# A hybrid SSD and pooling block: state products in plain fp32, silu in the convolution, inverse square roots as one GpSimd power

## The chip, the cores and the metric

The kernel runs on one core of one Trainium2 chip. The metric is the time on the device in microseconds (us), the median of three runs. The profile is of one further execution. Engines are named as in it: PE is TensorE (PEld its weight loads), DVE is VectorE, ACT is ScalarE, POOL is GpSimd, SP is SyncE, whose queue issues the loads.

## The reference

All arrays are fp32: 2048 latent tokens and 256 context tokens of 1024 channels. Cut to what matters here:

```python
x = layer_norm(x, emb_ln_g, emb_ln_b)
z, xbc, dt_raw, up = split_projection(modulate(x, sh1, sc1), in_proj)
xbc = silu(depthwise_conv_centred(xbc, conv_w, conv_b))     # x (1024), B (128), C (128)
# per direction, chunks of 128 tokens, 16 heads of 64:
y_diag = scores @ x                                         # inside a chunk
states = B^T (x * w_end);  h = h * chunk_decay + states     # from chunk to chunk
y_off  = (C h) * exp(a_cum)
y   = rms_norm((y_fwd + y_bwd + d_skip * x) * silu(z), ssd_norm_g)
mix = concat([y, pool_mixer(up)]) @ w_out
x   = layer_norm(ALPHA * x + g1 * mix, ln1_g, ln1_b)
ffn = (silu(h @ w_gate) * (h @ w_up)) @ w_down              # h = modulate(x, sh2, sc2)
x   = layer_norm(ALPHA * x + g2 * ffn, ln2_g, ln2_b)
```

The context goes through the same projection, convolution and scan first; its final states start the scans of the latent tokens.

## The kernel before

Nearly all products are made of three matmuls: each operand is split into a part rounded to fp32r and the rest, and `mm3` (L74) adds high times high, high times low and low times high. The split costs a cast on ACT and a subtraction on POOL or DVE for each operand. Plain fp32 products, one call of `mm` (L71) on unsplit operands, are used for the context's states and, in the scan, for chunks 0, 14 and 15 (`exact`, L1146).

The stages in order of time, with the rough stretch of the trace:

- 0 to 180 us: modulation rows, context, LayerNorms of the latent tokens (`ln_h`, L231) a step at a time between the blocks of a contraction. Each pair of token tiles needs one inverse square root (L247).
- 180 to 450 us: projection of B, C, dt and x. `x_block` (L805) makes a block of 128 channels for four groups of 512 tokens. `conv_main` (L594) copies the projection from PSUM (L601), `conv` (L368) makes the first tap on POOL (L373) and four more on DVE (L375), and on B, C and the context a silu on ACT (L377). The x blocks of the latent tokens go to `conv_tok` (L617) without silu, two blocks later, are transposed on PE and stored token-major in `xbc_d`. Beside the first two x blocks runs `dt_stage` (L766), which uses Exp on ACT.
- 450 to 840 us: u and its pooling, z, the decayed scores (`Scores`, L664).
- 840 to 1070 us, phase 2: from the last chunk to the first the pooled part of the output projection (48 matmuls of 512 columns a chunk, L1112) and the backward state. `prep` (L1065) loads x and B of the next chunk, applies silu (L1083, ACT), the end weights (L1084, POOL), and splits them (L1086 and L1087 on ACT, L1088 and L1089 on POOL). `add_state` (L385) makes two products a chunk.
- 1070 to 1510 us, phase 3: for every chunk `scan_y` (c+1), `scan_in` (c+2), `to_ffn` (c-1), `out_proj` (c). `scan_in` (L1142) loads C, x, the stored backward state, scores and z, applies silu to x (L1161), splits C, both states, B and the weighted x (L1152 to L1171, L1189 to L1192) and makes six products: two of `add_state`, and C times either state for each half of the channels (L1201, L1202). `scan_y` (L1210) adds the scores' product, gates, and splits y. `out_proj` (L1238) makes 48 matmuls, and needs two inverse square roots: of the mean square (L1251), without which its PSUM can't be emptied (L1252), and of the LayerNorm (L1258), without which the chunk can't go on to `to_ffn`.
- 1510 to 2500 us: gate and up projections as seven block products, prepared by ACT, POOL and DVE.
- 2500 us to the end: down projection; in its last sixteen slots of 33 matmuls each the second LayerNorm of a chunk (`finish`, L1576), with one inverse square root (L1583).

`rsqrt` (L82) is a guess from the exponent's bits and three Newton steps on tiles of one or two columns: eleven DVE instructions with one column (L88, L89, three times L94, twice L99, L102, L103), thirteen with two. There are 9 + 2 x 16 + 16 = 57 calls.

The tile framework orders each engine's instructions ahead of time from its own simulated timeline (`schedule_with_timeline_sim=True`, L1704), not as they are written. Engines work through their queues in that order. Buffers: in phase 3 three PSUM banks for `ps_mm`, two for transposes, three for `ps_ss`.

Of the kernel before, what the change touches and what calls it, by code (L numbers as in the profile page):

```python
# [21 lines left out]
H = 16  # L22
# [13 lines left out]
def hybrid_block_kernel(ctx: ExitStack, tc: tile.TileContext, a: dict, out: bass.AP, dbg=None):  # L36
# [45 lines left out]
    def rsqrt(v, n, tag):  # L82
        """[P, n] tile of v ** -0.5: a guess from the exponent bits and Newton's steps."""
        v_ = nc.vector
        i = small.tile([P, n], I32, tag=tag + "i", name=tag + "i")
        r = small.tile([P, n], F32, tag=tag + "r", name=tag + "r")
        t = small.tile([P, n], F32, tag=tag + "t", name=tag + "t")
        v_.tensor_scalar(out=i, in0=v.bitcast(I32), scalar1=1, scalar2=None, op0=ALU.logical_shift_right)  # L88
        v_.tensor_scalar(out=r.bitcast(I32), in0=i, scalar1=-1.0, scalar2=float(0x5F3759DF), op0=mult, op1=add)  # L89
        s = 1.0  # L90
        for step in range(3):
            # r is s times the guess, s a power of two
            if n == 1:
                v_.scalar_tensor_tensor(out=t, in0=r, scalar=v, in1=r, op0=mult, op1=mult)  # L94
            else:
                v_.tensor_tensor(out=t, in0=r, in1=r, op=mult)
                v_.tensor_tensor(out=t, in0=t, in1=v, op=mult)
            if step < 2:
                v_.scalar_tensor_tensor(out=r, in0=t, scalar=-3.0 * s * s, in1=r, op0=add, op1=mult)  # L99
                s = -2.0 * s ** 3  # L100
            else:
                v_.tensor_scalar(out=t, in0=t, scalar1=-0.5 / s ** 3, scalar2=1.5 / s, op0=mult, op1=add)  # L102
                v_.tensor_tensor(out=r, in0=r, in1=t, op=mult)  # L103
        return r
# [70 lines left out]
    class AdaRows:  # L175
        """Rows g * 2048 .. of the modulation as a chain of steps of kq blocks of the contraction."""
# [54 lines left out]
    def ln_h(src, t0, r, tp, parts, o, keep):  # L231
        """Two token tiles from row t0: columns o .. o+256 of the parts; a generator, a channel block at a time."""
# [84 lines left out]
    def atanh2(s, z, q):  # L317
        """s = 2 artanh(z), |z| <= 1/3, by its series; a generator, to be run a few instructions at a time."""
# [9 lines left out]
    def softplus(x, n, tp):  # L328
        """x [P, n, 32] <- softplus(x + dt_bias) = max(v, 0) + log1p(exp(-|v|)); a generator."""
# [38 lines left out]
    def conv(dst, raw, n, blk, act=True):  # L368
        """dst[:, j] = sum_d w[d] raw[:, j + d] + b for the 128 channels of block blk, then silu."""
# [6 lines left out]
        if act:  # L376
            nc.scalar.activation(out=dst, in_=dst, func=AF.Silu)  # L377
# [7 lines left out]
    def add_state(hn, hp, dec, xw, bt, low=None):  # L385
        """hn = hp * decay + B^T (x * w); both [P(n), 1024]; low: the operands' low parts."""
        if hp is not None:
            nc.vector.tensor_tensor(out=heads(hn), in0=heads(hp), in1=bch(dec), op=mult)
        for g in range(2):
            ps = ps_ss()  # L390
            s = slice(g * 512, (g + 1) * 512)
            if low is not None:
                mm3(ps, lambda k: bt, lambda k: low[1], lambda k: xw[:, s], lambda k: low[0][:, s], 1)
            else:
                mm(ps, bt, xw[:, s], True, True)
# [5 lines left out]
    # ==== phase 1: modulation, context, and the projections =====================================  # L401
# [58 lines left out]
    class Ahead:  # L460
        """The LayerNorms of the latent tokens, a step at a time, each one's loads and statistics during the one before."""
# [22 lines left out]
    def tick(n, m=0):  # L484
        """Every n blocks of a contraction, a step of the LayerNorms ahead."""
# [82 lines left out]
    def ctx_states():  # L568
        """The final states of the context's scans."""
# [24 lines left out]
    def conv_main(st, s, ps, blk):  # L594
# [14 lines left out]
        conv(cv[:, j0:j1], raw[:, j0:], j1 - j0, blk, blk >= 8)  # L609
# [54 lines left out]
    class Scores:  # L664
        """Both scans' decayed scores of the chunks, [j, (i block, h, i)], which depend on B, C and dt alone, and the skip.

        A product over 128 rows makes the exponents: running sums at i, what belongs to j, and the mask.
        Rows j >= 64 hold the block of their own i first.
        """
        def __init__(self, kp):  # L670
# [13 lines left out]
            # the skip's weight of each head where i is j, in the places of the scores  # L684
# [28 lines left out]
        def step(self):  # L713
            """Two groups of four heads."""
# [33 lines left out]
    def log(out_, x, tp):  # L748
        """out_ = ln x for x > 0: the exponent and 2 artanh((m - 1) / (m + 1)) of the mantissa m; a generator."""
# [16 lines left out]
    def dt_stage():  # L766
        with pool("dtp", "right") as dtp:
# [15 lines left out]
            for i in range(2):  # L783
                for d in range(2):
                    for half in range(2):
# [6 lines left out]
                        if i == 0:  # L792
                            # rows of the product, blocks of its columns, half of i
# [55 lines left out]
    def pool_block(u, w, ci):  # L849
# [20 lines left out]
        # rows  # L870
# [64 lines left out]
    def pooled_weights(w2s):  # L935
        """The pooling mixer's maps times the output projection's rows and the gate; a generator, in 16 blocks."""
# [89 lines left out]
    # modulation of the second sub-layer, folded with the first LayerNorm's affine part  # L1026
# [6 lines left out]
    # ==== phase 2: pooled part of the output projection; backward states =========================  # L1033
# [31 lines left out]
    def prep(c):  # L1065
# [9 lines left out]
        xh = xl = None  # L1075
        if c > 0:
            xl = b3.tile([P, D + P], F32R, tag=f"xt{c % 2}", name="xt")
            xt = f32(xl)
            if c >= NCH - 2:
                after(xl)  # L1080
# [627 lines left out]
```

## Time and profile before

| what | value |
|---|---|
| median of 3 runs | 2827.87 us (2825.07 to 2831.69) |
| profiled execution, its span from first to last instruction | 2824.6 us |
| PE busy | 2628.3 us, 93% of the span, 11886 matmuls |
| DVE busy | 1995.0 us, 71% |
| POOL busy | 1466.0 us, 52% |
| ACT busy | 979.3 us, 35% |
| DMA | 454.92 MB, mean 161 GB/s |

Of the profiled execution only the span is known, so its own time is taken as the span; the median of the runs lies 3.3 us above it. Busy shares are means over stages that differ. A matmul record's duration covers its way through the array, and records overlap, so what a matmul costs is read from the spacing of starts.

### The profile page before, as it was taken

The page shows a single profiled execution, that of the slowest core. Times are in us where ns is not written, and L with a number is a line of the kernel's source. Part 1 is how long each engine was busy: PE and PEld are TensorE (multiplying, and loading weights), DVE is VectorE, ACT ScalarE, POOL GpSimd, SP SyncE. Part 2 cuts the span into 40 slices and gives each one's busy share as a digit, 9 for nine tenths or more (in the row PEclk, how much of TensorE's full clock was granted, in tenths as well). Part 3 has the DMA queues.
Part 4 walks back from the last instruction along what each step waited for, and adds up shares of the span by engine and source line. Part 5 has one row for each costly group of instructions (what it writes and reads, how often), then busy time and mean ns, then how long its engine had stood idle before and what let it go on. Part 6 is the DMA issues. An engine that isn't in the chain of part 4 may idle for free.

```text
span 2824.6 us, 34660 instructions
## 1 busy us (share of the span) xinstructions
PE 2628.3 (93%) x11886; PEld 2091.9 (74%) x11886; DVE 1995.0 (71%) x2775; ACT 979.3 (35%) x1701; POOL 1466.0 (52%) x1177
## 2 busy tenths in 40 slices
PE   7989999999998898888898999998999998999996
PEld 3557788788876676666677888886888887888775
DVE  4767755856547886999988677678755555546787
ACT  2543221125533323444444322224333324333332
POOL 4554423424436786566644555555555553415366
PEclk9989999999999999999999999998999999999998
DMA  9722421137765666455565455545533327555643
GB/s 317 258 72 67 123 68 55 67 108 196 185 184 201 205 208 213 164 196 182 182 216 194 146 180 179 166 166 197 176 113 103 109 90 227 153 160 177 192 145 102
DMA packets 392456, 454.92 MB, mean 161 GB/s; under 512 B 31173, under 2 KB 287920, under 8 KB 388952
## 3 DMA queue, kind: packets, MB, share of 16 engines
q1 hardware_dynamic: 298016, 340.29, 38.7%
q10 hardware_dynamic: 93784, 112.30, 11.3%
q8 instruction: 94, 1.54, 0.2%
q14 instruction: 82, 0.67, 0.1%
q0 software_dynamic: 480, 0.11, 0.1%
HBM read 294.34 MB, written 158.28 MB: 160 GB/s over the span
## 4 chain that ended last, share of the span: by engine, by line
PE 29%; DVE 13%; issue 6%; POOL 4%; DMA 4%; ACT 2%; ACTq 0%; SPq 0%; POOLq 0%; DVEq 0%
PE b L72 28%; POOL x L1375 1%; DMA h<-hid_d 1%; PE mm L72 1%; DVE h L1415 1%; DVE h L1287 1%; DVE r2t L94 1%; DVE r1t L94 1%; POOL cs L1439 1%; DMA hid_d<-hs 1%; DVE xl L1192 1%; DVE sil L1235 1%; DVE ev L1388 1%; DMA wdr<-in_w_down 0%; DVE ryt L94 0%
## 5 line engine op out<-in xcount | busy, mean ns | idle before, releaser
L72 PE MATMUL b<-wd,h 128*128 128x512 f32 x1848 | 427.8, 394 | 16.5 <-ACT h L1414 7.6
L72 PEld LDWEIGHTS b<-wd,h 128*128 128x128 f32 x1848 | 351.1, 190 | 93.0 <-ACT h L1414 8.0
L72 PE MATMUL mm<-HT,wh 128*128 128x512 f32 x832 | 329.4, 398 | 3.8 <-ACT u L926 2.9
L72 PE MATMUL mm<-LT,wh 128*128 128x512 f32 x832 | 329.0, 395 | 0.0
L72 PE MATMUL mm<-HT,wl 128*128 128x512 f32 x832 | 327.7, 395 | 0.0
L1388 DVE TENSOR_TENSOR ev<-ev,b 128x512 f32<-128x512 f32 x301 | 200.8, 680 | 117.8 <-PE b L72 97.3
L1375 POOL TENSOR_TENSOR x<-cs,x 128x512 fp32r<-128x512 f32 x132 | 181.1, 1372 | 178.9 <-ACT x L1374 164.2
L1415 DVE TENSOR_TENSOR h<-h 128x768 fp32r<-128x768 f32 x112 | 134.9, 1214 | 125.5 <-ACT h L1414 121.0
L72 PEld LDWEIGHTS mm<-HT,wh 128*128 128x128 f32 x832 | 158.4, 190 | 38.2 <-ACT u L926 3.3
L72 PEld LDWEIGHTS mm<-LT,wh 128*128 128x128 f32 x832 | 158.1, 190 | 32.7 <-issue 0.7
L72 PEld LDWEIGHTS mm<-HT,wl 128*128 128x128 f32 x832 | 157.7, 189 | 32.8 <-issue 0.3
L1374 ACT CAST x<-cs 128x512 fp32r<-128x512 f32 x176 | 108.8, 621 | 184.0 <-PE b L72 67.5
L375 DVE SCALAR_TENSOR_TENSOR cv<-raw,vt,cv 128x512 f32<-128x512 f32 (+2 forms) x160 | 129.2, 819 | 59.7 <-POOL cv L373 56.8
L1375 POOL TENSOR_TENSOR x<-wraw,x 128x512 fp32r<-128x512 f32 x44 | 62.4, 1419 | 188.0 <-ACT x L1374 124.2
L1414 ACT CAST h<-h 128x768 fp32r<-128x768 f32 x112 | 87.0, 782 | 209.0 <-DMA h<-hid_d 186.8
L1374 ACT CAST x<-wraw 128x512 fp32r<-128x512 f32 x132 | 79.1, 620 | 187.5 <-PE b L72 98.8
L283 POOL TENSOR_TENSOR wl<-wraw,wh 128x1024 fp32r<-128x1024 f32 (+1 forms) x35 | 81.1, 2319 | 112.9 <-ACT wh L280 108.8
L72 PE MATMUL mm<-WyH,yh 128*128 128x512 f32 x256 | 109.2, 426 | 19.4 <-DVE bs L1252 16.7
L72 PE MATMUL b<-y0h,x 128*128 128x512 f32 x344 | 115.4, 397 | 5.5 <-ACT y0h L1334 5.5
L72 PE MATMUL b<-y1h,x 128*128 128x512 f32 x344 | 114.0, 393 | 3.6 <-ACT y1h L1334 3.6
L72 PE MATMUL b<-y4h,x 128*128 128x512 f32 x344 | 114.4, 394 | 0.0
L72 PE MATMUL b<-y3h,x 128*128 128x512 f32 x344 | 113.3, 390 | 0.0
(469 smaller groups left out, 6778.9 us busy)
## 6 DMA issues: line engine op xcount, KB each, us to landing
wraw<-in_w_gate SPq DMA_DIRECT2D x44, 512.0 KB
wraw<-in_w_up SPq DMA_DIRECT2D x44, 512.0 KB
hid_d<-ev ACTq DMA_DIRECT2D x88, 256.0 KB
h<-hid_d SPq DMA_DIRECT2D x56, 384.0 KB
tw_d<-wdr SPq DMA_DIRECT2D x77, 256.0 KB
wd<-tw_d SPq DMA_DIRECT2D x77, 256.0 KB
wada<-in_w_ada SPq DMA_DIRECT2D x72, 256.0 KB
wraw<-in_in_proj SPq DMA_DIRECT2D x35, 512.0 KB
```

What stands on the lines that cost most here:

```text
L72: nc.tensor.matmul(ps, lhsT=lhsT, rhs=rhs, start=start, stop=stop)
L94: v_.scalar_tensor_tensor(out=t, in0=r, scalar=v, in1=r, op0=mult, op1=mult)
L283: nc.gpsimd.tensor_tensor(out=wl[:, split:], in0=raw[:, split:], in1=f32(wh[:, split:]), op=sub)
L375: nc.vector.scalar_tensor_tensor(out=dst, in0=raw[:, d:d + n], scalar=w(d), in1=dst, op0=mult, op1=add)
L1192: nc.vector.tensor_tensor(out=xl, in0=xw, in1=f32(xh), op=sub)
L1235: nc.vector.tensor_reduce(out=sq, in_=y.rearrange("p k t -> p t k"), axis=mybir.AxisListType.X, op=add)
L1287: nc.vector.tensor_tensor(out=tt[i], in0=x, in1=y, op=sub)
L1374: nc.scalar.copy(h, src)
L1375: (nc.vector if i % 3 == 0 else nc.gpsimd).tensor_tensor(out=l, in0=src, in1=f32(h), op=sub)
L1388: nc.vector.tensor_tensor(out=o, in0=t, in1=ps, op=add)
L1414: nc.scalar.copy(th, f32(tl))
L1415: nc.vector.tensor_tensor(out=tl, in0=f32(tl), in1=f32(th), op=sub)
```

## The change

Three edits; comments and docstrings go too.

1. The state products of phases 2 and 3 take their operands unsplit, in plain fp32: `exact`, the splits and the low parts are gone. In `prep` the weighted x gets a buffer for even and one for odd chunks.
2. `conv` always ends in silu, so `xbc_d` holds silu of x, and the silus in `prep` and `scan_in` go.
3. `rsqrt` is one POOL instruction, a power with a constant tile of -0.5.

```diff
     def rsqrt(v, n, tag):
-        v_ = nc.vector
-        i = small.tile([P, n], I32, tag=tag + "i", name=tag + "i")
         r = small.tile([P, n], F32, tag=tag + "r", name=tag + "r")
...
+        nc.gpsimd.tensor_tensor(out=r, in0=v, in1=mhalf[:, 0:n], op=ALU.pow)
         return r
...
+    mhalf = cst.tile([P, 2], F32, name="mhalf")
+    nc.gpsimd.memset(mhalf, -0.5)
...
-        if act:
-            nc.scalar.activation(out=dst, in_=dst, func=AF.Silu)
+        nc.scalar.activation(out=dst, in_=dst, func=AF.Silu)
...
-            if low is not None:
-                mm3(ps, lambda k: bt, lambda k: low[1], lambda k: xw[:, s], lambda k: low[0][:, s], 1)
-            else:
-                mm(ps, bt, xw[:, s], True, True)
+            mm(ps, bt, xw[:, s], True, True)
...
-        conv(cv[:, j0:j1], raw[:, j0:], j1 - j0, blk, blk >= 8)
+        conv(cv[:, j0:j1], raw[:, j0:], j1 - j0, blk)
...
-            xs = b3.tile([P, D], F32, tag="xs", name="xs")
-            nc.scalar.activation(out=xs, in_=xt[:, 0:D], func=AF.Silu)
-            nc.gpsimd.tensor_tensor(out=heads(xs), in0=heads(xs), in1=bch(wend[:, c, H:2 * H]), op=mult)
-            xh = b3.tile([P, D + P], F32R, tag="xh", name="xh", bufs=1)
-            nc.scalar.copy(xh[:, 0:D], xs)
-            nc.scalar.copy(xh[:, D:D + P], xt[:, D:D + P])
-            nc.gpsimd.tensor_tensor(out=xl[:, 0:D], in0=xs, in1=f32(xh[:, 0:D]), op=sub)
-            nc.gpsimd.tensor_tensor(out=xl[:, D:D + P], in0=xt[:, D:D + P], in1=f32(xh[:, D:D + P]), op=sub)
+            xs = b3.tile([P, D], F32, tag=f"xs{c % 2}", name="xs")
+            nc.gpsimd.tensor_tensor(out=heads(xs), in0=heads(xt[:, 0:D]), in1=bch(wend[:, c, H:2 * H]), op=mult)
...
-        if not exact:
-            cth = se.tile([P, P], F32R, tag="cth", name="cth", bufs=2)
-            nc.scalar.copy(cth, ctk)
-            nc.gpsimd.tensor_tensor(out=ctl, in0=ctk, in1=f32(cth), op=sub)
-            hfh = so.tile([P, 2, 512], F32R, tag="y0h", name="hfh", bufs=2)
-            hfl = so.tile([P, 2, 512], F32R, tag="y0l", name="hfl", bufs=2)
-            h2 = hf.rearrange("p (g x) -> p g x", g=2)
-            nc.scalar.copy(hfh, h2)
-            nc.gpsimd.tensor_tensor(out=hfl, in0=h2, in1=f32(hfh), op=sub)
...
-        nc.scalar.activation(out=xt[:, 0:D], in_=xt[:, 0:D], func=AF.Silu)
...
-                xl = so.tile([P, 2, 512], F32R, tag="y0l", name="xl", bufs=2).rearrange("p g x -> p (g x)")
-                nc.scalar.copy(bh, xt[:, D:D + P])
-                nc.scalar.copy(xh, xw)
-                nc.vector.tensor_tensor(out=bl, in0=xt[:, D:D + P], in1=f32(bh), op=sub)
-                nc.vector.tensor_tensor(out=xl, in0=xw, in1=f32(xh), op=sub)
-                add_state(hn, hf, cdec[:, c, 0:H], xh, bh, (xl, bl))
+            add_state(hn, hf, cdec[:, c, 0:H], xw, xt[:, D:D + P])
...
-                mm3(pf, lambda k: cth, lambda k: ctl, lambda k: hfh[:, g], lambda k: hfl[:, g], 1)
-                mm3(pb, lambda k: cth, lambda k: ctl, lambda k: hbh[:, g], lambda k: hbl[:, g], 1)
+            mm(pf, ctk, hf[:, n], True, True)
+            mm(pb, ctk, hb[:, n], True, True)
```

## Rows read from the trace of the kernel before

**Rows 1.** Stretches: us, busy us (instructions) of PE, PEld, DVE, ACT, POOL, PEclk, DMA, GB/s
```profile
1186.00:1391.00 205.00, 171.72 (x925) 135.46 (x925) 197.38 (x319) 93.64 (x167) 130.49 (x79) 0.93 0.57 189
873.00:1046.00 173.00, 154.36 (x622) 122.25 (x621) 144.34 (x125) 51.66 (x77) 134.90 (x60) 0.94 0.61 208
250.00:450.00 200.00, 195.97 (x913) 157.08 (x912) 128.40 (x173) 49.21 (x100) 71.43 (x103) 1.00 0.32 89
620.00:830.00 210.00, 205.03 (x942) 168.79 (x941) 111.23 (x160) 104.19 (x214) 83.74 (x82) 0.99 0.67 186
```
**Rows 2.** Silus at the head of scan_in, ACT by time: start us, us
```profile
1186.62 1.05 ACT L1161 ACTIVATE xt<-xt 128x1024 f32<-128x1024 f32 x1
...
1391.12 1.07 ACT L1161 ACTIVATE xt<-xt 128x1024 f32<-128x1024 f32 x1
```
**Rows 3.** Waits of PE, 1186 to 1391 us: us in total, times, longest
```profile
PE mm L72 <- DVE bs L1252: 13.4, 6, 3.7
```
**Rows 4.** DVE groups, 1186 to 1391 us: busy us, mean ns, idle before
```profile
L1192 DVE TENSOR_TENSOR xl<-t,xh 128x1024 fp32r<-128x1024 f32 x8 | 18.1, 2260 | 0.0
L94 DVE SCALAR_TENSOR_TENSOR r1t<-r1r,ve 128x1 f32<-128x1 f32 x24 | 16.3, 677 | 0.7
...
L1191 DVE TENSOR_TENSOR bl<-xt,bh 128x128 fp32r<-128x128 f32 x8 | 5.5, 681 | 0.1
...
L88 DVE TENSOR_SCALAR ryi<-ssq 128x1 int32<-128x1 int32 x8 | 1.2, 148 | 0.1
```
**Rows 5.** A small DVE instruction beside a POOL one, by time: start us, us
```profile
1206.56 2.37 POOL L1171 TENSOR_TENSOR hbp<-hbp,hbh 128x1024 fp32r<-128x1024 f32 x1
1206.66 2.29 DVE L99 SCALAR_TENSOR_TENSOR ryr<-ryt,ryr 128x1 f32<-128x1 f32 x1
```
**Rows 6.** POOL groups, 1186 to 1391 us, then 873 to 1046 us
```profile
L1158 POOL TENSOR_TENSOR hfl<-hf,hfh 128x1024 fp32r<-128x1024 f32 x8 | 21.4, 2674 | 0.8 <-ACT hfh L1157 0.8
...
L1088 POOL TENSOR_TENSOR xt<-xs,xh 128x1024 fp32r<-128x1024 f32 x12 | 34.1, 2840 | 5.6 <-ACT xh L1086 5.6
```
**Rows 7.** PE by time: two plain fp32 products of the context's states (four records)
```profile
318.79 1.88 PE L72 MATMUL ss<-cxw,xtc 128*128 128x512 f32 x4
320.50 0.38 PE L624 MATMUL tr<-con,cv 128*128 128x128 f32 x2
```
**Rows 8.** PE by time: one split product (three records) and what follows it
```profile
1220.70 0.39 PE L72 MATMUL ss<-hfh,cth 128*128 128x512 f32 x1
...
1221.39 0.82 PE L1270 MATMUL tr<-con,bs 128*128 128x128 f32 x6
```
**Rows 9.** POOL, smallest arithmetic of two columns, whole span: busy us, mean ns
```profile
L252 POOL TENSOR_SCALAR stat<-nm 128x2 f32<-128x2 f32 x8 | 2.2, 281 | 5.3 <-DVE rst L96 2.7 <-DVE nm L249 2.5
```
**Rows 10.** PE by time, end of phase 3: waits in brackets
```profile
1486.27 1.97 PE L1270 MATMUL tr<-con,bs 128*128 128x128 f32 x8 [6.36 <-DVE ryr L89]
...
1512.72 1.41 PE L1270 MATMUL tr<-con,bs 128*128 128x128 f32 x8 [4.61 <-DVE bs L1259]
```
**Rows 11.** Waits of PE, 830 to 1070 us
```profile
PE ss L72 <- DVE hb L397: 8.5, 3, 3.4
PE ss L72 <- POOL xt L1088: 5.5, 4, 2.8
...
PE ss L72 <- ACT xh L1087: 2.7, 3, 1.1
```
**Rows 12.** The end of the kernel by time: last matmuls, then chunk 15's LayerNorm
```profile
2792.74 6.05 PE L72 MATMUL b<-wd,h 128*128 128x512 f32 x26
...
2809.50 0.68 DVE L1643 TENSOR_TENSOR acc<-acc,b 128x512 f32<-128x512 f32 x1
...
2816.31 0.21 DVE L1584 TENSOR_SCALAR nm<-mv,r2r 128x1 f32<-128x1 f32 x1
```
**Rows 13.** POOL in the last slots by time
```profile
2803.56 2.48 POOL L1588 TENSOR_TENSOR acc<-acc,ln_g_t 128x512 f32<-128x512 f32 x2 [2.02 <-ACT acc L1587]
```
**Rows 14.** ACT groups, 240 to 460 us: a silu of the convolution
```profile
L377 ACT ACTIVATE cv<-cv 128x514 f32<-128x514 f32 x1 | 0.6, 636 | 2.6 <-DVE cv L375 2.6
```

More of the change, by code (lines that the diff above doesn't have):

```diff
@@ L82, in rsqrt @@
     def rsqrt(v, n, tag):
-        v_ = nc.vector
-        i = small.tile([P, n], I32, tag=tag + "i", name=tag + "i")
         r = small.tile([P, n], F32, tag=tag + "r", name=tag + "r")
[L87 to L94, printed above, removed]
-            else:
[L96 to L103, printed above, removed]
+        nc.gpsimd.tensor_tensor(out=r, in0=v, in1=mhalf[:, 0:n], op=ALU.pow)
         return r
@@ L366, in ssd_coef, with conv @@
         nc.scalar.activation(out=cd, in_=v, func=AF.Exp)
-    def conv(dst, raw, n, blk, act=True):
+    def conv(dst, raw, n, blk):
         def w(d):
@@ L383, in bch, with add_state @@
         return ap.unsqueeze(2).broadcast_to([P, n, m])
-    def add_state(hn, hp, dec, xw, bt, low=None):
+    def add_state(hn, hp, dec, xw, bt):
         if hp is not None:
@@ L1096, in prep @@
         nc.gpsimd.tensor_tensor(out=x, in0=x, in1=ab, op=add)
-        return (xh, xl), dh, dl, x
+        return xs, xt, dh, dl, x
     cur = prep(NCH - 1)
@@ L1101, in hybrid_block_kernel @@
         rows_c = slice(c * P, (c + 1) * P)
-        xhl, dh, dl, x = cur
+        xs, xt, dh, dl, x = cur
         if c > 0:
@@ L1145, in scan_in @@
         sc = sq_ if c % 2 else se
-        exact = c == 0 or c >= 14
-        ctl = se.tile([P, P], F32R, tag="ctl", name="ctl", bufs=2)
-        ctk = f32(ctl)
+        ctk = se.tile([P, P], F32, tag="ctk", name="ctk", bufs=2)
         load(ctk, ct_d[:, rows_c])
-        if not exact:
-            cth = se.tile([P, P], F32R, tag="cth", name="cth", bufs=2)
-            nc.scalar.copy(cth, ctk)
-            nc.gpsimd.tensor_tensor(out=ctl, in0=ctk, in1=f32(cth), op=sub)
-            hfh = so.tile([P, 2, 512], F32R, tag="y0h", name="hfh", bufs=2)
-            hfl = so.tile([P, 2, 512], F32R, tag="y0l", name="hfl", bufs=2)
-            h2 = hf.rearrange("p (g x) -> p g x", g=2)
-            nc.scalar.copy(hfh, h2)
-            nc.gpsimd.tensor_tensor(out=hfl, in0=h2, in1=f32(hfh), op=sub)
         xt = sc.tile([P, D + P], F32, tag=f"xt{c % 2}", name="xt")
         load(xt, xbc_d[rows_c, :])
-        nc.scalar.activation(out=xt[:, 0:D], in_=xt[:, 0:D], func=AF.Silu)
         hb = hb_0
         if c:
-            hbl = (sq_ if c % 2 else sr).tile([P, D], F32R, tag=f"hb{c % 2}", name="hbp")
-            hb = f32(hbl)
+            hb = (sq_ if c % 2 else sr).tile([P, D], F32, tag=f"hb{c % 2}", name="hbp")
             load(hb, hb_d[rows_c, :])
-        if not exact:
-            hbh = so.tile([P, 2, 512], F32R, tag="y0h", name="hbh", bufs=2)
-            hbl = hbl.rearrange("p (g x) -> p g x", g=2)
-            nc.scalar.copy(hbh, f32(hbl))
-            nc.gpsimd.tensor_tensor(out=hbl, in0=f32(hbl), in1=f32(hbh), op=sub)
         wt = sc.tile([P, 4, 2, 4, 64], F32, tag=f"wt{c % 2}", name="wt")
@@ L1182, in scan_in @@
             hn = se.tile([P, D], F32, tag="hf", name="hf", bufs=2)
-            if exact:
-                add_state(hn, hf, cdec[:, c, 0:H], xw, xt[:, D:D + P])
-            else:
-                bh, bl = (se.tile([P, P], F32R, tag="b" + n, name="b" + n) for n in "hl")
-                xh = se.tile([P, D], F32R, tag="xh", name="xh")
-                xl = so.tile([P, 2, 512], F32R, tag="y0l", name="xl", bufs=2).rearrange("p g x -> p (g x)")
-                nc.scalar.copy(bh, xt[:, D:D + P])
-                nc.scalar.copy(xh, xw)
-                nc.vector.tensor_tensor(out=bl, in0=xt[:, D:D + P], in1=f32(bh), op=sub)
-                nc.vector.tensor_tensor(out=xl, in0=xw, in1=f32(xh), op=sub)
-                add_state(hn, hf, cdec[:, c, 0:H], xh, bh, (xl, bl))
+            add_state(hn, hf, cdec[:, c, 0:H], xw, xt[:, D:D + P])
         for g in range(2):
```

14 lines of the change are left out of this document (4 added, 10 removed).

## The prediction

> **What bounds the kernel now.** I read the busy times by stretch first. In the x projection and in the score stage PE is busy for 98% of the time with DVE at 64% and 53%: PE is the bound there. In the steady part of phase 3 it is DVE: 197.4 of 205 us busy, 96%, PE 84% at a granted clock of 0.93 [rows 1]. Phase 2 is mixed: PE 89%, DVE 83%, POOL 78% [rows 1]. Then the waits. In the steady part of phase 3 PE waits longest for L1252, the DVE instruction that empties PSUM once the inverse square root is there [rows 3]. Two single waits at the end of phase 3 sit behind the square roots too, 6.4 and 4.6 us [rows 10]. In phase 2 PE waits for DVE's L397 and for the split of x [rows 11]. At the end PE stops at 2798.8, and chunk 15's PSUM is read only at 2809.5, because DVE is still in the square roots of the chunks before [rows 12].
>
> The period of a chunk in phase 3 is (1391.12 - 1186.62) / 8 = 25.6 us [rows 2].
>
> **Phase 3, what leaves DVE.** In those eight chunks L1192 takes 18.1 us, L1191 5.5 us, and the eleven groups of the two square roots, from 16.3 us down to 1.2 us, add up to 59.8 us [rows 4]. That is 83.4 of 197.4 us; 114 us or 14.3 us a chunk are left. One thing may help further, and I don't price it: a DVE instruction of one column took 2.29 us beside a POOL instruction of 2.37 us [rows 5], and POOL loses the splits L1158 and L1171, 21.4 us each, and L1153, 4.2 us [rows 6], so it goes from 130.5 to 83.5 us, 10.4 a chunk, and the powers. ACT loses casts and silu and has room anyway (93.6 of 205 us).
>
> **Phase 3, what PE gains in work.** A split product takes 1221.39 - 1220.70 = 0.69 us [rows 8], a plain one (320.50 - 318.79) / 2 = 0.855 us [rows 7], so each plain product costs 0.165 us more. Six a chunk: 1.0 us. What PE needs a chunk at full clock: at a mean of 0.93, with levels of 1.2 and 2.4 GHz, 14% of the stretch ran at the lower one, 28.7 us, of which half would go. (171.7 - 14.4) / 8 = 19.7 us, and with the plain products 20.7 us.
>
> **Phase 3, the sum.** PE is now the longest at 20.7 us, DVE next at 14.3, POOL at 10.4 and two powers. The bound isn't reached for free: 19.7 of 25.6 us is 77% now, the score stage, with DVE at 53%, reaches 98%. DVE at 14.3 of some 22 us, 64%, is near that stage, so I take 92%: 22.4 us a chunk. Bounds: 21.1 us (98%) and 24.5 us (85%, between). 13 chunks (1 to 13) have split operands now: 13 x (25.6 - 22.4) = 41 us, bounds 14 and 58. The two waits at the end, 11.0 us [rows 10], shrink by what a power is faster than eleven instructions; I take 7 us, bounds 0 and 11.
>
> **The power itself** is in no row. From below it costs what POOL's smallest arithmetic on two columns costs, 0.28 us [rows 9], from above what the longest plain POOL instruction does, 2.84 us [rows 6]. I take 1.0 us, since it has the small one's shape but more to do. The step moves from DVE to POOL, and POOL works in order: it waits at the power for L1250, L1257 or L1582, and behind it stand L1181, L1207, L1230 and L1232 of other chunks, for which the transposes, the split of y and so PE wait. With POOL under 60% and a planner that knows the order, that is part of the 92%. If the cover is gone, a power is exposed twice a chunk, some 2 us, which the 24.5 us hold.
>
> The Trainium skill (Perfetto Trace Analysis, Optimizing Scalar/DVE Operations) says that GPSIMD and DVE share an SBUF read port, so that moving operations from one to the other might not help. The trace agrees about the port [rows 5]: the small instruction took as long as POOL's. By that rule the square roots would bring nothing; DVE would lose the two subtractions alone. That is one of the rivals, worked out below from rows.
>
> **Phase 2.** Silu, casts and both POOL subtractions go: L1088 alone takes 2.84 us a chunk [rows 6]. Of PE's waits those for the split, 5.5 + 2.7 = 8.2 us, go; what is late next is the weighting L1084, without a silu ahead of it, so it starts earlier. The wait for L397, 8.5 us [rows 11], I halve: DVE keeps its instructions, but POOL's load falls. The 30 plain products cost 30 x 0.165 = 5.0 us. 8.2 + 4.3 - 5.0 = 8 us (7.5), bounds -5 (all waits stay) and 20 (the lost clock, 0.94, comes back too).
>
> **The end.** The square root stands between L1643 at 2809.50 and L1584 at 2816.31 [rows 12]. With a power, DVE needs few instructions a slot and has emptied the slot before in time, so L1643 comes at about 2799; 0.68 + 0.69 of statistics and 0.5 of small ones, a power, and L1584 is at 2802 instead of 2816.3. What follows it, 2824.6 - 2816.3 = 8.3 us, stays. That would be 14 us; but POOL has L1588 and L1589, a pair of 2.48 us each, for every chunk in the last slots [rows 13], and some of that stands ahead of the power. I take 11 us, bounds 4 and 14. DVE relief at the change of operands in the down projection: 3 us, bounds 0 and 6.
>
> **Silu in the convolution** adds 32 ACT instructions of 0.64 us, 20 us [rows 14], and a few table loads where Exp comes between in the first two blocks. ACT is busy for 49 of 200 us there [rows 1], the transposes come two blocks later, and the silu waits in ACT's queue for DVE's L375 with the next copy from PSUM (L601) behind it, which four PSUM banks cover. I cost it at nothing; without cover it is 20 us. The 9 square roots of the first LayerNorms I cost at nothing: a power takes the place of thirteen DVE instructions; even at 2.84 us each they are 26 us of POOL's time in the first 180 us. The 57 powers add no DMA, and no queue of SP is touched.
>
> **Sum.** 41 + 7 + 8 + 11 + 3 = 70 us off a span of 2824.6 gives 2754.6; the median stands 3.3 us above the span: 2758 us.
>
> **The rivals.**
> - *Fuller.* PE reaches 98% of phase 3 as in the score stage: 58 + 9 + 18 + 13 + 5 = 103 us, 2725 us. For it: DVE at 64% and POOL near 55% are no higher than elsewhere beside a full PE. Against: phase 2, where PE had 89%.
> - *The chain instead of the load.* Phase 3 stays near 24.5 us, because PE's order is fixed and each chunk's PSUM still waits for a power behind POOL's queue; phase 2 gives nothing, the end 8 us, its waits 4: 14 + 4 + 8 = 26 us, 2802 us. For it: PE's waits are for single instructions [rows 3]; against: DVE had no slack at all, so each wait carried the queue ahead of it. If the move between DVE and POOL brought nothing, DVE would keep (197.4 - 18.1 - 5.5) / 8 = 21.7 us a chunk, near 23.5 us with a little idle: 13 x 2.1 + 8 + 4 = 39 us, 2789 us. This is the port rule's case.
> - *Silu uncovered.* The forecast with 20 us back: 2778 us.
> - *A slow power, the slower side.* The place is the last sixteen slots. A slot has 33 matmuls at 0.23 us, 7.6 us; POOL has twice 2.48 us of its own there, L1588 and L1589 [rows 13], so each us of a power above 2.6 us adds 16 us, and in the scan POOL's 10.4 + two powers pass 22.4 us from 6 us on. At p us the balance is 8 + 13 x (15.2 - 2p) + 11 - 16 x (p - 2.6), which is nothing at about 6 us; from there it is slower. At 8 us: 8 - 10 + 11 - 86 = -77, 2905 us. Against: POOL's arithmetic on two columns takes 0.28 us [rows 9].
>
> **How the numbers follow.** Forecast (2735 to 2785, the silu case and the port case's edge in it) 0.56; fuller 0.18; chain and port 0.18; slow power 0.08. The range has to hold 8 in 10: 2715 to 2808 takes in most of the fuller case and of the chain's, and leaves out the slow power. About 0.2%, 5.7 us, can be told from no change. Faster by more: forecast, fuller, and nearly all of the chain: 0.89. Same: 0.03, from the tail of the chain and a power at the balance. Slower: 0.08.
>
> **What would show it.** The period between two heads of scan_in near 22.4 us, DVE at 60 to 70% there, PE over 90%; plain products 0.855 us apart; PE's waits for L1252 down to a few us; L1643 of chunk 15 within 2 us of the last matmul. Wrong: a power whose row is several us, or PE waiting behind POOL in phase 3; PE below 95% between 250 and 450 us would bring the silu case.

## The result and the profile after

The changed kernel takes 2765.4 us (median of four runs, 2756.4 to 2770.3) against 2826.5 us for the kernel before on the same chip: a ratio of 0.977 (95% interval 0.975 to 0.979). The forecast was 2758 us. The profiled execution has a span of 2762.7 us, 61.9 us less than before; the forecast's sum was 70 us. That the total lies near the forecast hides two misses of opposite sign, which the experiments below take apart: the change itself brings 81 us of span (78 us by the medians), and some 19 us of it (18 by the medians) are lost again to something that the prediction did not look at, the addresses of tiles that the change does not touch. That the two nearly cancel is luck.

The page after, its first two rows and the chain that ended last, share of the span by engine:

```profile
span 2762.7 us, 33705 instructions
PE 2649.9 (96%) x11778; PEld 2053.4 (74%) x11778; DVE 1767.3 (64%) x2209; ACT 913.3 (33%) x1611; POOL 1371.5 (50%) x1166
...
PE 80%; DMA 6%; DVE 5%; POOL 3%; issue 3%; ACT 2%; SPq 0%; ACTq 0%; POOLq 0%; DVEq 0%
```

Four fifths of the chain is now PE's own work. Stretches after, with the columns of [rows 1] (us; busy us and instructions of PE, PEld, DVE, ACT, POOL; PEclk; DMA; GB/s): the x projection, phase 2, the steady part of phase 3, the down projection.

```profile
250.00:450.00 200.00, 196.30 (x895) 154.81 (x894) 121.80 (x166) 72.79 (x135) 64.86 (x101) 0.99 0.31 87
850.00:1070.00 220.00, 202.61 (x791) 152.54 (x790) 155.96 (x153) 26.52 (x45) 110.71 (x45) 0.95 0.61 203
1150.00:1350.00 200.00, 200.00 (x1054) 143.31 (x1054) 145.19 (x194) 75.79 (x152) 118.15 (x92) 1.00 0.75 243
2344.00:2444.00 100.00, 100.00 (x436) 81.50 (x435) 57.93 (x73) 34.59 (x53) 41.05 (x28) 1.00 0.56 173
```

In phase 3 PE is busy for 200.00 of 200 us at the full granted clock, where it was 84% at 0.93 [rows 1]; DVE fell from 96% to 73%. The silus of z, one a chunk, give the period (instructions, ns, first and last start in us):

```profile
L1131 ACT ACTIVATE sz<-sz x11: 1042/1059/1064, 1160.3 to 1363.1; 128x1024 f32<-128x1024 f32 x11
```

(1363.1 - 1160.3) / 10 = 20.3 us a chunk, against 25.6 us [rows 2]. The heads of `scan_in` run ahead there, so the pace of a chunk is read better from PE's own work, the first matmul with WyH of chunks 7 and 13 (start us, us):

```profile
1269.96 0.79 PE L72 MATMUL mm<-WyH,yh 128*128 128x512 f32 x1
...
1373.36 0.79 PE L72 MATMUL mm<-WyH,yh 128*128 128x512 f32 x1
```

(1373.36 - 1269.96) / 6 = 20.7 us. From chunk 2, which starts at 1138.49, it is 234.9 / 11 = 21.4 us, against 26.3 us before (1140.28 to 1430.00). The power that replaces Newton's steps, by its four uses (ns shortest/median/longest; start of first and last):

```profile
L85 POOL TENSOR_TENSOR ryr<-ssq,mhalf x16: 544/549/998, 1126.5 to 1416.5; 128x1 f32<-128x1 f32 x16
L85 POOL TENSOR_TENSOR r1r<-ve,mhalf x16: 542/549/1479, 1135.4 to 1424.7; 128x1 f32<-128x1 f32 x16
L85 POOL TENSOR_TENSOR r2r<-ve,mhalf x16: 542/1078/1132, 2632.9 to 2753.5; 128x1 f32<-128x1 f32 x16
L85 POOL TENSOR_TENSOR rsr<-ve,mhalf x9: 692/749/1171, 13.9 to 169.7; 128x2 f32<-128x2 f32 x9
```

So 0.55 to 1.1 us at the median, with 1.0 us forecast. What it replaces has to be counted again: the DVE instructions that the description of `rsqrt` lists for one column are 1 + 1 + 3 + 2 + 1 + 1 = nine, not eleven, and with two columns twelve, not thirteen. The pages of the profile agree: DVE goes from 2775 to 2209 instructions, and 48 x 9 + 9 x 12, with the 26 subtractions of L1191 and L1192, are 566. The 59.8 us that the prediction adds up is a sum over rows (twelve groups, not eleven) and stands. The page before, its second row:

```profile
PE 2628.3 (93%) x11886; PEld 2091.9 (74%) x11886; DVE 1995.0 (71%) x2775; ACT 979.3 (35%) x1701; POOL 1466.0 (52%) x1177
```

PE's longest wait at the end of phase 3 (1380 to 1440 us) and in phase 2 (845 to 1075 us), as in [rows 3] (us in total, times, longest):

```profile
PE tr L1211 <- DVE bs L1200: 4.2, 1, 4.2
...
PE ss L72 <- DVE hb L377: 17.4, 5, 6.1
```

The waits for L1252 [rows 3] are gone. In phase 2 the waits for the split of x [rows 11] are gone as well, but the wait for DVE's state, 8.5 us before [rows 11], has doubled.

Where the time went, by stretch, in the profiled executions of before, of the changed kernel, and of the changed kernel with all left-hand tiles back at their old addresses (the first experiment). Phase 2 runs from its first to its last matmul with W2H, phase 3 to the last matmul with WyH, the FFN from the first to the last ev, the down projection to the start of the last record of PE with wd, the tail to the end (the first record of PE with wd stands at 2354 us before and at 2298 us after, so the down projection begins there and not at 2500 us, as the list of stages has it):

| stretch | before | after | after, old addresses | forecast gain | gain after | gain at old addresses |
|---|---|---|---|---|---|---|
| to the first u | 445.5 | 443.3 | 439.8 | 0 | 2.2 | 5.7 |
| to phase 2 | 402.0 | 406.2 | 404.5 | 0 | -4.2 | -2.5 |
| phase 2 | 229.9 | 228.6 | 228.3 | 8 | 1.3 | 1.6 |
| phase 3 | 399.2 | 337.3 | 335.6 | 41 + 7 | 61.9 | 63.6 |
| to the first ev | 11.5 | 9.6 | 10.2 | 0 | 1.9 | 1.3 |
| FFN | 873.6 | 880.6 | 869.7 | 0 | -7.0 | 3.9 |
| down projection | 436.7 | 439.7 | 434.5 | 3 | -3.0 | 2.2 |
| tail | 26.2 | 17.4 | 20.7 | 11 | 8.8 | 5.5 |
| span | 2824.6 | 2762.7 | 2743.3 | 70 | 61.9 | 81.3 |

Among all kernels run here whose FFN and addresses are those of before, the FFN took 869.7 to 879.8 us, so a row of a few us says little by itself; the pace of PE within it is the surer measure.

### The profile page after: what moved, and what is told of

Read it like the earlier page. It is cut to its first block, busy times and chain, and to the rows that moved or that the text cites. A ratio compares the mean times of both kernels' runs of the same rounds, so it can differ in the third digit from the quotient of the medians.

```text
span 2762.7 us, 33705 instructions
## 1 busy us (share of the span) xinstructions
PE 2649.9 (96%) x11778; PEld 2053.4 (74%) x11778; DVE 1767.3 (64%) x2209; ACT 913.3 (33%) x1611; POOL 1371.5 (50%) x1166
## 4 chain that ended last, share of the span: by engine, by line
PE 80%; DMA 6%; DVE 5%; POOL 3%; issue 3%; ACT 2%; SPq 0%; ACTq 0%; POOLq 0%; DVEq 0%
PE b L72 42%; PE mm L72 30%; PE ss L72 6%; DVE cv L359 1%; DMA wada<-in_w_ada 1%; POOL acc L1530 1%; DMA base_d<-bx 1%; POOL acc L1529 1%; PE tr L1161 1%; PE tr L604 1%; PE tr L246 0%; DMA dl<-dp_d 0%; DMA lnx<-in_x 0%; DMA bx<-in_x 0%; PE tr L1211 0%
## 5 line engine op out<-in xcount | busy, mean ns | idle before, releaser
L72 PE MATMUL b<-wd,h 128*128 128x512 f32 x1848 | 433.9, 397 | 13.4 <-ACT h L1355 7.4
L72 PEld LDWEIGHTS b<-wd,h 128*128 128x128 f32 x1848 | 349.5, 190 | 97.6 <-DVE wd L1344 8.0
L1356 DVE TENSOR_TENSOR h<-h 128x768 fp32r<-128x768 f32 x112 | 125.8, 1131 | 155.0 <-ACT h L1355 154.8
L72 PE MATMUL mm<-WyH,yh 128*128 128x512 f32 x256 | 115.6, 451 | 1.9 <-ACT yh L1172 1.9
```

The source lines that it names most:

```text
L72: nc.tensor.matmul(ps, lhsT=lhsT, rhs=rhs, start=start, stop=stop)
L1356: nc.vector.tensor_tensor(out=tl, in0=f32(tl), in1=f32(th), op=sub)
```

## The experiments

### The addresses

After the change PE's 512-column matmuls are further apart everywhere, in stages too where no instruction changed: by stretches of 200 us from 200 to 2800 us, the median spacing is 227 ns before and 231 to 234 ns after. In 100 us of the down projection, at a granted clock of 1.00 both times, before held 443 matmuls and after 436 (last row of the stretches above); the stretch of before, same columns:

```profile
2400.00:2500.00 100.00, 100.00 (x443) 82.84 (x442) 61.12 (x75) 36.53 (x56) 43.23 (x28) 1.00 0.58 176
```

What differs there is where tiles lie. The scratch tiles of Newton's steps are gone from the pool `small` (512 bytes a partition), the constant -0.5 adds 32 bytes, and so the first tile on the left side of SBUF moves from byte 26336 to 25856. On the right side tiles of phases 2 and 3 move by multiples of 512 bytes, and the others stay.

The first two kernels move tiles and change no instruction:

```diff
-    mhalf = cst.tile([P, 2], F32, name="mhalf")
+    mhalf = small.tile([P, 2], F32, tag="mhalf", name="mhalf", bufs=1)
+    small.tile([P, 120], F32, tag="pad", name="pad", bufs=1)      # changed kernel, 480 bytes
...
+    small.tile([P, 8], F32, tag="pad", name="pad", bufs=1)        # kernel before, 32 bytes
```

> The changed kernel with 480 bytes a partition of padding, so that every tile on the left side of SBUF lies where it lay in the kernel before (first left tile at byte 26336; in the changed kernel it is 25856, because the square root's scratch tiles are gone). No instruction differs. Theory A (addresses set the pace of PE): the 512-column matmuls come 227 ns apart again, as in the kernel before, instead of 231 to 234 ns; some 10,000 of them by 4 ns are 40 us, so about 2725 us. Theory B (the pace differs by chip or execution): 231 to 234 ns stays or changes for all kernels of this call alike, and the time is that of the changed kernel, about 2765 us.

> The kernel before with 32 bytes a partition of padding: every tile on the left side of SBUF moves up by 32 bytes (first left tile at 26368 in place of 26336), nothing else differs. Theory A (addresses set the pace of PE): matmuls 231 to 234 ns apart instead of 227 ns, about 2865 us. Theory B (chip or execution): 227 ns and about 2827 us, no change.

Measured: 2747.8 us for the changed kernel at the old addresses, ratio to before 0.971 (0.969 to 0.973), spacing 227 ns; 2847.4 us for the kernel before moved by 32 bytes, 1.0065 (1.005 to 1.008), spacing 231 to 234 ns. Theory A holds in direction and pace, in both kernels, on one chip; the time moved by half of what I had worked out (18 and 21 us instead of 40), because not every matmul is affected.

Which place is a good one? Two more paddings, 448 and 416 bytes:

> The changed kernel with 448 instead of 480 bytes of padding: the first left tile lies at byte 26304, a multiple of 64 and not of 128. If what counts is a multiple of 64, matmuls are 231 to 234 ns apart and the time is about 2765 us; if only multiples of 128 are slow (25856 and 26368 are such), 227 ns and about 2748 us.

> The changed kernel with 416 bytes of padding: first left tile at byte 26272, which is 32 past a multiple of 64, like 26336, but 32 instead of 96 past a multiple of 128. If the place within 64 bytes counts: matmuls 227 ns apart, about 2748 us; if the place within 128 bytes counts: 231 to 234 ns, about 2765 us.

Measured: 2760.7 us (231 to 233 ns) and 2762.4 us (228 to 233 ns), one run each. Neither rule holds as I put it: of the four places 0, 32, 64 and 96 past a multiple of 128, only 96 is fast. But the right-hand tiles lie at 96 too. So I set each of the 5460 matmuls of the FFN and the down projection beside the addresses of its two operands, and took the spacing to the next one (those of 200 to 300 ns; place within 128 bytes of the streamed operand and of the weights):

```
kernel             streamed / weights   count   mean ns   median ns
before                  96 / 96          5378     226.8     227
changed                  0 / 0           1418     228.2     227
changed                  0 / 96          1028     233.0     234
changed                 96 / 0           1618     233.3     234
changed                 96 / 96          1326     228.2     227
448 bytes padding       64 / 64          1419     228.7     227
448 bytes padding       64 / 96          1020     233.3     234
448 bytes padding       96 / 64          1620     233.3     234
416 bytes padding       32 / 32          1419     228.9     227
416 bytes padding       32 / 96          1035     233.3     233
416 bytes padding       96 / 32          1625     229.8     229
```

Products whose operands lie at the same place have the median of before, whichever place it is (in the kernels with one side moved their mean is 1 to 2 ns higher); those with unequal places take 6 to 7 ns more (96 / 32 only 3). That was read off afterwards, so it needed a run that could fail: both sides at 64, with 32 bytes on the right besides the 448 on the left.

```diff
+    padr = ctx.enter_context(pool("padr", "right"))
+    padr.tile([P, 8], F32, name="padr")
```

> The changed kernel with the left tiles at byte 26304 (as in the run with 448 bytes of padding, 64 past a multiple of 128) and 32 bytes of padding at the top of SBUF as well, so that the tiles on the right side move down by 32 bytes, from 96 to 64 past a multiple of 128. Both operands of nearly every product then lie at the same place within 128 bytes again, though at another one than in the kernel before. Theory E (what counts is whether the two operands lie at the same place within 128 bytes): matmuls 227 ns apart, about 2748 us, as at the addresses of the kernel before. Theory F (96 past a multiple of 128 is the fast place, 0, 32 and 64 are slow ones): 231 ns or more, about 2765 us or more.

Measured: 2751.1 us, 0.974 (0.972 to 0.976); 5377 products at 64 / 64, mean 226.7 ns. 200 us of the FFN, columns as above, with the left side alone at 64:

```profile
2000.00:2200.00 200.00, 200.00 (x868) 162.58 (x867) 108.83 (x148) 63.37 (x106) 107.59 (x78) 1.00 0.31 102
```

and with both sides at 64:

```profile
2000.00:2200.00 200.00, 200.00 (x884) 165.62 (x883) 111.08 (x151) 62.91 (x105) 108.20 (x79) 1.00 0.32 104
```

868 matmuls against 884, with no instruction changed (869 in the changed kernel, 884 in it at the old addresses): the pace follows whether the operands' places agree. Theory E stands. The weights of the next product count too: 64 products of the changed kernel have equal places of their own and the next weights at the other place, and their median is 235 ns, while the same 64 take 227 ns at the old addresses (235 ns also with the left side at 64, but 226 to 227 with it at 32). Streaming and weight loads run at the same time (PEld is busy for 81.50 of 100 us in which PE is busy for 100, last row of the stretches after). That the two reads get in each other's way is an inference from this; the runs don't settle it, since the 63 products with unequal places of their own and the next weights at the place of the streamed operand are slow as well (28 of them at a median of 230.5 ns, 35 at 235).

### What held phase 3: one part alone, and a load that nobody waits for

The square roots alone (the kernel before with `rsqrt` as in the change, padded so that no address differs), and the products of phase 3 alone:

```diff
-        exact = c == 0 or c >= 14
+        exact = True
```

> One part alone: the kernel before with the inverse square roots as GpSimd powers (padded, so that no address differs); products with states stay split, silu of x stays where it was. Theory L (DVE's load held phase 3): DVE keeps (197.4 - 59.8) / 8 = 17.2 us a chunk, PE 19.7, POOL 16.3 plus two powers, 17.8 us: a period of about 22 us instead of 25.6, 13 x 3.6 = 47 us, with 7 at the end of phase 3 and 9 in the tail: about 2765 us. Theory P (moving work from DVE to GpSimd brings nothing, since they hold each other up): phase 3 stays at 25.6 us a chunk and only the tail gains, 9 us: about 2818 us.

> One part alone: the kernel before with the products of phase 3 whose operand is a state in plain fp32 without splits; phase 2, the square roots by Newton's steps and the silu stay. Theory L (DVE's load): DVE loses L1191 and L1192, 23.6 / 8 = 2.95 us, and keeps 21.7 us a chunk; the period falls to about 23.5 us, 13 x 2.1 = 27 us: about 2800 us. Theory P (the splits, not the square roots, hold phase 3, because POOL's and DVE's splits hold each other up): most of what the whole change gave in phase 3, some 50 to 60 us: about 2770 us.

Measured: powers alone 2762.2 us, 0.977 (0.975 to 0.979), phase 3 349.5 us; plain products alone 2779.4 us, 0.982 (0.980 to 0.984), phase 3 346.6 us. Each alone takes some 50 us off phase 3; both together (with the silu moved) take 64, not 100. The powers came out as theory L had them; the plain products gave nearly twice (47 us) what its sum over DVE's own instructions allowed. Their stretch from 1186 to 1391 us:

```profile
1186.00:1391.00 205.00, 196.19 (x1030) 139.46 (x1029) 182.07 (x363) 79.91 (x151) 98.17 (x69) 0.99 0.67 217
```

and two of Newton's DVE groups in it, those that changed most (busy us, mean ns, idle before):

```profile
L94 DVE SCALAR_TENSOR_TENSOR r1t<-r1r,ve 128x1 f32<-128x1 f32 x28 | 13.1, 468 | 0.9
...
L99 DVE SCALAR_TENSOR_TENSOR ryr<-ryt,ryr 128x1 f32<-128x1 f32 x20 | 3.2, 158 | 0.6
```

The same instructions on one column, which nothing has changed, take 468 ns instead of 677 [rows 4]; all 288 of Newton's in phase 3 take 86 us instead of 120, some 2 us a chunk less. POOL has lost the splits that ran beside them (POOL 98 us of 205 instead of 130), and that this is the cause shows in phase 3 of the kernel before, instruction by instruction: the 119 with two tensor operands that run beside no POOL instruction take 0.22 us at most, the 73 that run beside one 1.15 us on average, and those with one tensor operand take 0.15 us either way. With plain products only 49 run beside one. It is what [rows 5] showed at one place and the forecast left unpriced. And PE is at 96%: from here PE is the bound, so the second part can't bring its 50 us again.

Was it DVE's load, or the wait at the end of a chain of small instructions? The powers alone, with the small instructions put back, eighteen a chunk (the expectation says 22), where nobody waits for them:

```diff
+        for t in "uv":
+            burden(mv[:, 1:2], 1, t)      # Newton's DVE instructions, into scratch
         store(x1_d[rows_c, :], bs)
```

> The kernel before with powers (as in the run of the power alone), and with the 22 small DVE instructions a chunk that Newton's steps used in phase 3 put back as a burden: they run on scratch columns after the LayerNorm's statistics, and nothing waits for what they give. Addresses as before. Theory L (DVE's load held phase 3): the load is back, so phase 3 goes from 349.5 us (power alone) back to about 399, and the time to about 2812 us. Theory W (it was the wait: PSUM is emptied only after the last of a chain of small instructions): nobody waits for these, so phase 3 stays near 350 us and the time near 2765.

Measured: 2806.7 us, 0.993 (0.991 to 0.994), phase 3 388.0 us: 38.5 of the 49.7 us that the powers had gained are lost again. Stretch 1150 to 1350 us, powers alone:

```profile
1150.00:1350.00 200.00, 183.65 (x1044) 146.12 (x1043) 170.60 (x201) 103.76 (x185) 156.18 (x107) 0.97 0.67 218
```

and with the burden:

```profile
1150.00:1350.00 200.00, 168.82 (x922) 135.08 (x922) 185.54 (x319) 93.43 (x168) 139.05 (x95) 0.92 0.58 188
```

PE falls from 184 to 169 of 200 us as DVE rises from 171 to 186. DVE's load was the cause for at least three quarters. The load did not come back whole: between the first WyH matmuls of chunks 2 and 13 DVE is busy for 24.9 us a chunk before, 18.0 with powers and 23.0 with the burden, 5.0 of 6.9 us. So the other 11 us can be load too; what the wait itself was worth is not shown.

### Silu alone

```diff
-        conv(cv[:, j0:j1], raw[:, j0:], j1 - j0, blk, blk >= 8)
+        conv(cv[:, j0:j1], raw[:, j0:], j1 - j0, blk)
...
-            nc.scalar.activation(out=xs, in_=xt[:, 0:D], func=AF.Silu)
...
-        nc.scalar.activation(out=xt[:, 0:D], in_=xt[:, 0:D], func=AF.Silu)
```

> One part alone: the kernel before with silu of x in the convolution and none in phases 2 and 3; the splits and Newton's steps stay, no address differs. The forecast costed it at nothing: 2826 us, with some 2 or 3 us more up to the first u (the runs with it reached u 2 to 3 us later than those without) given back in phase 2 or 3. If silu in the convolution is not covered: 20 us more up to the first u, about 2846 us. If the silu at the head of scan_in was part of what held phase 3: phase 3 below 395 us and the time below 2820 us.

Measured: 2826.6 us, 1.000 (0.999 to 1.001); the first u at 444.6 us (445.5 before), phase 3 397.9 us. The silu is covered where it was moved to, and was in nobody's way where it was.

### Phase 2

In the changed kernel PE waits for DVE's state (L377). DVE by time in phase 2 (start us, us; wait in brackets):

```profile
904.39 0.68 DVE L1086 TENSOR_TENSOR bx<-bx,mm 128x512 f32<-128x512 f32 x1
910.92 0.81 DVE L1067 TENSOR_SCALAR bx<-bx,stat 128x1024 f32<-128x1024 f32 x1 [5.85 <-DMA bx<-in_x]
```

and the waits of SP's queue from 850 to 1070 us (us in total, times, longest):

```profile
SPq L63 <- DMA base_d<-bx: 76.7, 12, 8.9
SPq L63 <- DVE WyL L1098: 61.7, 12, 8.0
```

DVE stands in front of L1067 for the load of `bx`, with L377 of the state behind it. The load is late because SP, in order, waits until the old rows in that buffer are stored (76.7 us in total) and until L1098 frees the only buffer of raw `w_out` rows (61.7 us). So I gave both three buffers, in the changed kernel at the old addresses; the room comes from weighting x in place:

```diff
-            xs = b3.tile([P, D], F32, tag=f"xs{c % 2}", name="xs")
+            xs = xt[:, 0:D]
...
-        x = (b3 if c % 2 else bp).tile([P, D], F32, tag=f"bx{c % 2}", name="bx")
+        x = b3.tile([P, D], F32, tag="bx", name="bx", bufs=3)
...
-                raw = b3.tile([P, 512], F32, tag="wyraw", name="wyraw")
+                raw = b3.tile([P, 512], F32, tag="wyraw", name="wyraw", bufs=3)
```

> The changed kernel at the addresses of the kernel before (2747.8 us), with other buffers in phase 2: three for the base rows instead of one for even and one for odd chunks, three for the raw rows of w_out instead of one; the room comes from weighting x in place. No work is added. Theory S (phase 2 stayed at 228.3 us because the loads in SP's queue wait: 82 us in total for the store of the base rows, 62 us for L1099, which frees the raw rows, and DVE and PE then wait behind DVE's queue): PE needs 16 x 10.9 + 30 x 0.855 = 200 us, so phase 2 falls to 205 to 215 us, and the time to about 2730 us. Theory D (DVE's own order or the chain of states): phase 2 stays at about 228 us, 2748 us.

Measured: 2751.2 us, 0.972 (0.971 to 0.974), no gain, though phase 2 fell from 228.3 to 215.4 us. Most of the 13 us came back right behind it: phase 3 takes 347.1 instead of 335.6 us. PE's wait between 1040 and 1110 us:

```profile
PE ss L72 <- POOL t L1137: 14.5, 1, 14.5
```

SP by time at that place, where it had stood 15.7 us for the store of base rows:

```profile
1062.86 0.81 SPq L63 DMA_DIRECT2D bs<-base_d  x2
1063.76 0.38 SPq L63 DMA_DIRECT2D hf<-hf  x1
```

The load of the base rows waits for their store, and phase 3's first state (hf), C and x stand behind it. The last kernel of this line moves those loads back, and takes over the mended tail of the next section:

```diff
+        if c < 3:
+            nc.gpsimd.tensor_copy(bs[:, 0:1], sq[:, 0:1])
         load(bs, base_d[rows_c, :])
```

> The changed kernel at the addresses of the kernel before, with the buffers of phase 2 of the earlier run, the second half's scaling on DVE, and one thing new: the loads of the base rows of the first three chunks of phase 3 wait for that chunk's sums of squares, so that in SP's queue they stand behind the loads of the first states, C, x and scores instead of ahead of them. Theory S (the 13 us that the buffers brought in phase 2 were given back because SP stood 15.7 us at a base load that waits for the store of the same rows): phase 2 at about 215 us and no gap behind it, 2741 - 13 = about 2728 us. Theory G (phase 3's first loads are late for another reason): the gap of about 14 us at the start of phase 3 stays, about 2740 us.

Measured: 2740.1 us, 0.969 (0.967 to 0.971); phase 2 214.4 us, phase 3 339.6 us. PE's gap shrank from 14.5 to 9.7 us, not to nothing, and the total equals that of the mended tail alone. SP still waits 13.6 us for a store of base rows there, now with the first x of phase 3, whose tile lies in the room of phase 2's buffers. Theory S holds for phase 2 and G for the time: the loads between the two phases are the next bound.

### The tail

The end of the changed kernel by time, PE, DVE and POOL:

```profile
2735.77 9.85 PE L72 MATMUL b<-wd,h 128*128 128x512 f32 x42
...
2747.44 0.22 DVE L1525 TENSOR_SCALAR nm<-mv,r2r 128x1 f32<-128x1 f32 x1 [4.71 <-POOL r2r L85]
2747.57 0.68 DVE L1584 TENSOR_TENSOR acc<-acc,b 128x512 f32<-128x512 f32 x1
...
2754.04 0.21 DVE L1525 TENSOR_SCALAR nm<-mv,r2r 128x1 f32<-128x1 f32 x1 [4.64 <-POOL r2r L85]
...
2748.58 2.48 POOL L1529 TENSOR_TENSOR acc<-acc,ln_g_t 128x512 f32<-128x512 f32 x2 [1.18 <-ACT acc L1528]
2751.02 2.48 POOL L1530 TENSOR_TENSOR acc<-acc,ln_b_t 128x512 f32<-128x512 f32 x2
2753.46 0.55 POOL L85 TENSOR_TENSOR r2r<-ve,mhalf 128x1 f32<-128x1 f32 x1
```

The power takes 0.55 us, but it stands in POOL's order behind both pairs of the chunk before, so DVE waits 4.6 to 4.8 us for it in each of the last slots. At the old addresses PE is faster and the lag is longer: the last matmul ends at 2699.70 + 23.28 = 2722.98 us, and chunk 15's PSUM is emptied 5.2 us later.

```profile
2699.70 23.28 PE L72 MATMUL b<-wd,h 128*128 128x512 f32 x102
...
2728.19 0.68 DVE L1585 TENSOR_TENSOR acc<-acc,b 128x512 f32<-128x512 f32 x1
```

With one half of each pair moved to DVE, in the changed kernel at the old addresses:

```diff
-            for (i, x), e in ((h1, V if c == NCH - 1 else G), (h0, G)):
+            for (i, x), e in ((h1, V), (h0, G)):
```

> The changed kernel at the addresses of the kernel before, and with the scaling of one of the two halves of every chunk's second LayerNorm (the instructions L1530 and L1531 of the half h1) on DVE instead of GpSimd. Theory Q (the power of a chunk waits in GpSimd's queue behind two pairs of 2.5 us of the chunk before, so that GpSimd sets 6.7 us a slot and DVE empties PSUM 5.2 us after the last matmul): GpSimd keeps 2.5 + 0.55 us a slot, PSUM of chunk 15 is emptied within 1 us of the last matmul, and the tail after the last matmul goes from 20.7 to about 15.5 us: about 2743 us. Theory R (the tail is the chain of chunk 15's own LayerNorm and store): 20.7 us stays.

Measured: 2741.1 us, 0.969 (0.968 to 0.971); the tail goes from 20.7 to 12.5 us. The last rows of DVE and POOL there:

```profile
2720.93 0.68 DVE L1585 TENSOR_TENSOR acc<-acc,b 128x512 f32<-128x512 f32 x1
...
2724.01 0.21 DVE L1526 TENSOR_SCALAR nm<-mv,r2r 128x1 f32<-128x1 f32 x1 [1.24 <-POOL r2r L85]
...
2723.43 0.55 POOL L85 TENSOR_TENSOR r2r<-ve,mhalf 128x1 f32<-128x1 f32 x1
```

PSUM of chunk 15 is emptied 0.4 us after the end of the last matmul (2720.52) instead of 5.2 us, and DVE waits 1.2 us for the power. Theory Q holds. This kernel and the last one of phase 2 are the best of those tried, 0.9% below the changed kernel; 18 of these 24 us are addresses.

## Why the prediction was right and where it was wrong

- *Phase 3, mechanism right, term too small (48 forecast, 62 measured).* DVE's load was the bound and the two parts took it away: DVE does 145.19 / 200 x 21.4 = 15.5 us a chunk (14.3 forecast), POOL 12.6 (10.4 and two powers). The step that was off is "I take 92%": PE is busy for 200.00 of 200 us, and a chunk takes 21.4 us where 22.4 were forecast; the bound of 98% stood at 21.1. PE's need of 20.7 us was right: it is what a chunk takes from chunk 7 on. So of the 62 us, 55 lie between chunks 2 and 13 (289.7 - 234.9), where 41 were forecast for 13 chunks. The price of a plain product was right: one starts at 1199.86 and PE's next instruction at 1200.72, 0.86 us.

```profile
1199.86 1.02 PE L72 MATMUL ss<-hf,ctk 128*128 128x512 f32 x2
1200.72 0.27 PE L1211 MATMUL tr<-con,bs 128*128 128x128 f32 x1
```

- *The rival "chain instead of load" is refuted:* a chunk takes 21.4 us, not 24.5, and instructions that nobody waits for take 38.5 of the 49.7 us back. So is the port rule's case: the powers alone bring 64 us where it gave 39 for the whole change. The Trainium skill (Perfetto Trace Analysis, Optimizing Scalar/DVE Operations) says that GPSIMD and DVE share an SBUF read port, so that moving operations between the two might not help. The port is seen here (468 against 677 ns as POOL's load falls), but the conclusion does not follow when nine instructions become one of 0.55 us: then most of the work is removed, not moved.
- *The waits at the end of phase 3* went from 11.0 [rows 10] to 4.2 us: 6.8 us against 7 forecast, right.
- *Phase 2: wrong (8 forecast, about 1 measured).* The step that failed: the waits for the split go, the weighting is late next, and the wait for the state is halved. The split's waits went, and the wait for the state grew from 8.5 to 17.4 us, for the lateness that they showed came from SP's queue: loads behind a store and behind a buffer of one. Take one instruction out of a chain that starts with a late load, and the next one waits for the same load. The profile of before had it in SP's own waits, 850 to 1070 us, which I had not read:

```profile
SPq L63 <- DVE WyL L1125: 80.5, 13, 9.0
SPq L63 <- DMA base_d<-bx: 60.1, 12, 9.2
```

- *The tail: size near (11 forecast, 8.8), reason half right.* L1584 does come 2.0 us after the last matmul, as the forecast had it; but at the old addresses, with the faster PE, it is 5.2 us and the gain 5.5. The power was late by POOL's order, of which the forecast had counted only "some". With POOL relieved the tail gives 13.7 us, near the upper bound of 14.
- *Down projection: 3 forecast, -3 measured;* at the old addresses 2.2. A relief is not shown: at the old addresses the down projection takes 434.5 to 438.7 us with powers and 436.7 to 437.8 without. The addresses took 5.2 us.
- *Silu in the convolution at nothing:* right. PE 196.30 of 200 us (195.97 before [rows 1]) with ACT up from 49 to 73 us.
- *The LayerNorms' square roots at nothing:* a little low. The two kernels with powers and the old silu reach the first u at 436.7 and 438.4 us, the two without powers at 445.5 and 443.0 us: some 5 to 9 us gained.
- *Not in the prediction at all: addresses,* -19.4 us of span (2743.3 - 2762.7). Dropping scratch tiles was counted as DVE work alone.

## What to carry to other kernels

Read the queue of the loads (SP's own waits) before crediting a removed step with the wait that it ended: a wait names the last link of a chain, and a late load passes on to the next link. When a change removes or adds a tile, compare the addresses of all matmul operands before and after, and hold them by padding when measuring the change. Two parts that relieve the same engine don't add up once PE is full; price the second against the bound that the first leaves.

## What the runs showed of the hardware that was not expected

- The pace of 512-column fp32r matmuls at full granted clock depends on where the two operands lie within 128 bytes of each other: 227 ns at equal places (0, 32, 64 and 96 seen), 233 to 234 ns at unequal ones (229 to 230 ns for 96 / 32). On this kernel that is 18 to 21 us of 2800. The Trainium skill (SBUF — State Buffer, SBUF: two separate sides) says that within the engine side only the pair of ports shared by DVE and GpSimd causes contention, and that PE never waits on anyone. By that alone the pace of PE would not hang on where its operands lie; here it does, and the measurement decides.
- A GpSimd power on one column takes 0.54 to 0.57 us with DVE idle beside it; 15 of the 48 take 0.93 to 1.48 us, all of them beside a DVE instruction.
- A DVE instruction of one column with two tensor operands takes 0.14 to 0.22 us with no POOL instruction beside it and 1.15 us on average beside one (phase 3 of the kernel before); one with a single tensor operand takes 0.15 us either way. So a chain of nine costs DVE 59.8 / 16 = 3.7 us.
